# Seven-product merge and output projections in a one-core hybrid mixer layer

## The chip, the core and the metric

The kernel runs on one NeuronCore of a Trainium2 chip. The metric is device time in microseconds (us). Five engines matter here: TensorE multiplies matrices (PE in the profile; its weight loads are PEld), VectorE (DVE) and ScalarE (ACT) do elementwise work and read TensorE's results out of PSUM, GpSimd (POOL) takes some small work, and SyncE (SP) issues nearly all DMAs, in order.

## What is computed

One layer with width 1024 and sequence length 1024, all in float32, is computed transposed: channels lie on partitions, time on the free dimension.

```
h   = rms_norm(x, g) * (1 + scale(c)) + shift(c)        # scale, shift: rows of silu(c) @ ada_w
z   = h @ w_in                                          # q,k,v,z of three mixers + 3 x 1024 gate logits
y_b = mixer_b(z) * silu(z_b)                            # stick-breaking (sb), gated DeltaNet (gdn), GLA
m   = sum over b of sigmoid(gate_b) * (y_b @ proj_b)    # y_sb, y_gdn 512 wide, y_gla 1024 wide
out = x + gate(c) * (m @ w_out)
```

DeltaNet and GLA normalise their output per head with a learned scale (the "onorm" scale) ahead of the multiplication with silu(z_b).

## The kernel before, in words

**Exactness.** A float32 operand is cut into a high and a low part (`split`, L149: ScalarE rounds the high part at L151, VectorE subtracts at L152; with a column of scales L154 and L155 do it). A product is three matmuls: high·high, high·low, low·high. One matmul of the dense work takes a 128x128 stationary block and streams 128x512 through it. So a projection of 128 output channels with 1024 inputs over 1024 time steps costs 2 halves × 8 × 3 = 48 matmuls, one with 512 inputs 24 (`run_cm`, L187).

**Start.** The squares of x are summed over partitions by matmuls with ones (`add_up`, L316); VectorE adds some pairs first (L322, L329, L334). Two ScalarE steps (L336, L337) make the RMS factor `rstd`. The conditioning rows scale and shift of channel block k come for k = 0, 1 from 32 one-column matmuls on TensorE (`by_product`, L360, added up at L366), for k = 2 to 7 from VectorE reductions of an `ada_w` tile with silu(c) (`by_rows`, L369; L372, L374). Then for each k VectorE scales x (L404), ScalarE makes `h_hi` (L407) and VectorE `h_lo` (L409), and TensorE runs a block of 24 matmuls (eight accumulators in eight PSUM banks) on it while the next k is made.

**Middle.** `emit` (L247) weaves the three mixers, written as tasks with the names of what must be done before them, into a list of dense groups that fills TensorE's gaps. Of the 24 merge gates (3 branches × 8 blocks) 18 are computed early (`EARLY`, `FILL`, `early_gate`, L220) and stored in `g_dram`; they are fetched again later. The mixers store y in `y_dram`.

**Final stage** (`final_groups`, L1310). Eight GLA projections over the first 512 inputs are copied to `merged`. Then for GLA's second half, gdn and sb: eight projections each (`proj_group`, L1257), between them the gates, fetched or computed (six of them here). VectorE multiplies by the gate and adds into `merged` (L1267 to L1272). With the sb branch `merged` is split into `m_hi`, `m_lo`, and eight output projections follow (`out_group`, L1288): VectorE adds x (L1303), SyncE stores (L1306). The onorm scales are put into the projection weights: 96 pairs of L154/L155 on 128x128 pieces. `wp` holds three raw weight tiles and three split tiles.

## Time and profile before

| | us |
|---|---|
| Three runs | 1512.1, 1510.86, 1512.94; median 1512.1 |
| Profiled execution | 1507.79, of which the span is 1506.0 |
| TensorE busy | 1467.5 of 1506.0 |
| VectorE / ScalarE / GpSimd busy | 844.5 / 679.5 / 150.5 |
| Mean granted TensorE clock | 0.99 of full speed |

The span is the time between the first and the last instruction; 1.8 us of the execution lie around it. TensorE's busy time is from modelled ends, and consecutive matmuls overlap in the records, so the price of a matmul is read from the distance between starts, not from its length. In rows of the timeline the bracket gives the engine's idle time just before and what ended it.

### The profile page before, as it was taken

The page shows a single profiled execution, that of the slowest core. Times are in us where ns is not written, and L with a number is a line of the kernel's source. Part 1 is how long each engine was busy: PE and PEld are TensorE (multiplying, and loading weights), DVE is VectorE, ACT ScalarE, POOL GpSimd, SP SyncE. Part 2 cuts the span into 40 slices and gives each one's busy share as a digit, 9 for nine tenths or more (in the row PEclk, how much of TensorE's full clock was granted, in tenths as well). Part 3 has the DMA queues.
Part 4 walks back from the last instruction along what each step waited for, and adds up shares of the span by engine and source line. Part 5 has one row for each costly group of instructions (what it writes and reads, how often), then busy time and mean ns, then how long its engine had stood idle before and what let it go on. Part 6 is the DMA issues. An engine that isn't in the chain of part 4 may idle for free.

```text
span 1506.0 us, 26643 instructions
## 1 busy us (share of the span) xinstructions
PE 1467.5 (97%) x10628; PEld 1235.0 (82%) x10628; DVE 844.5 (56%) x1838; ACT 679.5 (45%) x1471; POOL 150.5 (10%) x295
## 2 busy tenths in 40 slices
PE   7998999989999999999999999999999999999998
PEld 4887777777778888879788999889988888888887
DVE  4978647476643756667576525563556226474621
ACT  5367645453743747465577423341433442322200
POOL 1021232133321000000000100000000000000000
PEclk8999999999999999999999999999999999999999
DMA  7634332131330212121122121111122234353442
GB/s 272 187 101 123 94 86 61 50 90 33 104 90 27 54 50 71 29 57 44 53 57 65 50 64 43 50 42 50 35 83 92 86 104 140 119 154 112 117 142 77
DMA packets 162470, 126.48 MB, mean 84 GB/s; under 512 B 23429, under 2 KB 139269, under 8 KB 162346
## 3 DMA queue, kind: packets, MB, share of 16 engines
q1 hardware_dynamic: 162202, 124.47, 28.6%
q8 instruction: 83, 1.36, 0.4%
q14 instruction: 41, 0.34, 0.1%
q10 hardware_dynamic: 144, 0.31, 0.1%
HBM read 99.80 MB, written 24.95 MB: 83 GB/s over the span
## 4 chain that ended last, share of the span: by engine, by line
PE 83%; DVE 8%; ACT 3%; DMA 3%; POOL 2%; issue 2%; SPq 0%; POOLq 0%; DVEq 0%; ACTq 0%
PE acc L95 66%; PE lv L95 7%; PE mx L95 6%; PE tr L122 2%; DVE u L436 1%; PE tr L95 1%; DVE w L621 1%; DVE w L623 1%; DVE w L152 1%; POOL w L647 1%; POOL c L284 1%; DMA w<-ad 1%; DMA w<-xd 1%; DVE u L1161 1%; DMA u<-in_xT 0%
## 5 line engine op out<-in xcount | busy, mean ns | idle before, releaser
L95 PE MATMUL acc<-h_hi,w 128*128 128x512 f32 x1856 | 656.4, 408 | 0.0
L95 PEld LDWEIGHTS acc<-h_hi,w 128*128 128x128 f32 x1856 | 352.0, 190 | 70.2 <-issue 0.2
L95 PE MATMUL acc<-h_lo,w 128*128 128x512 f32 x928 | 365.3, 394 | 1.8 <-DVE h_lo L409 1.8
L95 PEld LDWEIGHTS acc<-h_lo,w 128*128 128x128 f32 x928 | 176.8, 190 | 29.2 <-DVE h_lo L409 2.3
L95 PE MATMUL acc<-whi,h_hi 128*128 128x256 f32 x640 | 186.8, 292 | 0.0
L95 PE MATMUL acc<-wlo,h_hi 128*128 128x256 f32 x640 | 180.7, 282 | 0.0
L95 PE MATMUL acc<-whi,h_lo 128*128 128x256 f32 x640 | 180.7, 282 | 0.0
L95 PE MATMUL acc<-u,w 128*128 128x512 f32 x768 | 176.5, 391 | 0.0
L95 PEld LDWEIGHTS acc<-u,w 128*128 128x128 f32 x768 | 144.1, 188 | 31.7 <-ACT v L1226 0.2
L151 ACT CAST w<-raw 128x512 fp32r<-128x512 f32 x144 | 84.9, 619 | 131.8 <-PE acc L95 90.4
L152 DVE TENSOR_TENSOR w<-raw,w 128x512 fp32r<-128x512 f32 x144 | 97.5, 688 | 46.5 <-ACT w L151 46.0
L95 PEld LDWEIGHTS acc<-whi,h_hi 128*128 128x128 f32 x640 | 122.3, 191 | 1.4 <-issue 0.7
L95 PEld LDWEIGHTS acc<-wlo,h_hi 128*128 128x128 f32 x640 | 122.5, 191 | 0.1
L95 PEld LDWEIGHTS acc<-whi,h_lo 128*128 128x128 f32 x640 | 122.2, 191 | 0.0
L284 POOL TENSOR_TENSOR c<-c,mhalf 128x4 f32<-128x4 f32 (+1 forms) x56 | 55.0, 982 | 582.8 <-DVE c L282 581.4
L95 PE MATMUL acc<-m_hi,w 128*128 128x512 f32 x256 | 79.1, 389 | 0.0
L1161 DVE TENSOR_TENSOR_SCAN u<-u,zero_c 128x128 f32<-128x128 f32 (+7 forms) x32 | 43.4, 1356 | 35.5 <-ACT u L1159 35.5
L155 DVE SCALAR_TENSOR_TENSOR w<-raw,col,w 128x128 fp32r<-128x128 f32 x96 | 29.5, 349 | 55.7 <-ACT w L154 48.9
L95 PEld LDWEIGHTS mx<-r,u 128*128 128x128 f32 x288 | 44.1, 190 | 18.1 <-DVE r L802 5.2
L95 PEld LDWEIGHTS acc<-m_hi,w 128*128 128x128 f32 x256 | 48.1, 188 | 10.1
L95 PE MATMUL mx<-r,u 128*128 128x128 f32 x288 | 48.4, 280 | 6.3 <-POOL u L771 2.3
L95 PE MATMUL lv<-u,u 128*32 128x32 f32 (+5 forms) x528 | 48.9, 251 | 2.6 <-DVE u L704 2.6
(258 smaller groups left out, 2154.7 us busy)
## 6 DMA issues: line engine op xcount, KB each, us to landing
raw<-in_w_in SPq DMA_DIRECT2D x160, 256.0 KB, 3.0
g_dram<-v SPq DMA_DIRECT2D x36, 256.0 KB, 2.1
v<-g_dram SPq DMA_DIRECT2D x36, 256.0 KB, 2.7
u<-in_xT SPq DMA_DIRECT2D x16, 512.0 KB, 4.7
u<-y_dram SPq DMA_DIRECT2D x16, 512.0 KB, 3.7
ada<-in_adaT SPq DMA_DIRECT2D x12, 512.0 KB, 5.2
u<-in_adaT SPq DMA_DIRECT2D x8, 512.0 KB, 4.0
v<-gam_d SPq DMA_DIRECT2D x16, 256.0 KB, 3.6
```

The lines of the kernel that those rows point to most:

```text
L95: return nc.tensor.matmul(out, lhsT=lhsT, rhs=rhs, **kw)
L122: nc.tensor.transpose(out=out, in_=in_, identity=ident[:k, :k])
L151: nc.scalar.copy(out=hi, in_=raw)
L152: nc.vector.tensor_sub(out=lo, in0=raw, in1=hi.bitcast(F32))
L155: nc.vector.scalar_tensor_tensor(out=lo, in0=raw, scalar=scale, in1=hi.bitcast(F32), op0=ALU.mult, op1=ALU.subtract)
L284: nc.gpsimd.tensor_tensor(out=out, in0=out, in1=mhalf[:, 0:n], op=ALU.pow)
L436: nc.vector.scalar_tensor_tensor(out=t, in0=r[:, tap:tap + T], scalar=C("conv", j + tap), in1=t, op0=ALU.mult, op1=ALU.add)
L621: nc.vector.tensor_tensor(out=t3, in0=L3[:, w:16, j:w].broadcast_to([32, n, w]), in1=Xl3[:, j:w, 0:w].broadcast_to([32, n, w]), op=ALU.mult)
L623: nc.vector.tensor_sub(out=Xl3[:, w:16, 0:w], in0=Xl3[:, w:16, 0:w], in1=t3)
L647: nc.gpsimd.tensor_scalar(out=dst[:, :, 16 * e:16 * e + 16], in0=c3, scalar1=K("par")[:, e:e + 1], scalar2=None, op0=ALU.mult)
L1161: nc.vector.tensor_tensor_scan(om[:, 0:n][:, ::-1], om[:, 0:n][:, ::-1], zero_c.broadcast_to([P, n]), 1.0, ALU.mult, ALU.add)
```

## The change

Lines of the changed program are named with "new".

- **Seven products.** Output blocks p and p + 4 of the GLA projection, and of the output projection, are made together. With weights and inputs seen as 2x2 blocks (inputs 0 to 511 and 512 to 1023; time halves), seven block products in Winograd's form replace eight. VectorE forms s1 to s4 from the raw weights (`part`, new L1264 to L1272) and each is split; the input side has the units b11, t1, t2, b22, t3, b21, t4. A unit is 12 matmuls; two PSUM banks X and W take turns, and a bank is read in the middle of its accumulation (`read`) ahead of the unit after the next.
- **Input sums.** GLA's t1 to t4 are formed by four tasks `T.y` in the middle of the program: 16 loads of 128x512 from `y_dram`, 16 VectorE subtractions, 16 stores. Those of the output projection are formed from `merged` between the sb projections (`out_operands`, new L1449).
- **Final order.** All 24 gates go through `g_dram`. The six late ones come first in the final stage, then four GLA pairs, 16 gdn and sb projections in alternation, four output pairs. Operands are loaded into the low half's place and split there (`load_unit`, `load_y`).
- **Onorm scales** are multiplied in when y is made (40 instructions become scalar_tensor_tensor with a scalar column); the 96 pairs of L154/L155 on weights go.
- **Start.** All conditioning rows by VectorE, two more reductions for each of k = 0, 1; one more VectorE addition of squares (new L339, L340) and two ones-matmuls fewer; eight products of a constant with ones whose result nothing reads (`keep_busy`), three ahead of the squares and five behind them.
- Weight tiles: six of half the size, eight raw tiles instead of three.

```diff
-EARLY = [(g, d) for g in (1, 0, 2) for d in range(2, KT)]
+EARLY = [(g, d) for g in (1, 0, 2) for d in range(KT)]
...
-    wp = ctx.enter_context(tc.tile_pool(name="wp", bufs=3))
+    wp = ctx.enter_context(tc.tile_pool(name="wp", bufs=6))
...
+    idle = bank(pt, "tr", HALF)
+
+    def keep_busy(n):
+
+        for _ in range(n):
+            mm(idle, ones, cst[:, 0:HALF], 858, start=True, stop=True)
+
+    keep_busy(3)
...
-        return wp.tile([P, 4, P], F32, tag="raw", name="raw")
...
+        return wp.tile([P, 4, P], F32, tag="raw", name="raw", bufs=8)
+
+    def w_tile():
+        return wp.tile([P, 2, 4, P], F32R, tag="w", name="w")
...
+    def load_half(hi, lo, src, k0):
+        split(hi, lo, load_raw(src, k0))
+
+    def load_w(src, kt=KT):
+        ws = []
         for k0 in range(0, kt, 4):
-            load_half(w[:, 0, k0:k0 + 4, :], w[:, 1, k0:k0 + 4, :], src, k0, scales)
-        return w
+            w = w_tile()
+            load_half(w[:, 0], w[:, 1], src, k0)
+            ws.append(w)
+        return ws
...
-    nc.vector.tensor_add(out=low[1], in0=low[1], in1=low[2])
-    add_up(low[1], start=True)
-    add_up(low[0])
+    nc.vector.tensor_add(out=low[0], in0=low[0], in1=low[1])
+    nc.vector.tensor_add(out=low[0], in0=low[0], in1=low[2])
+    add_up(low[0], start=True)
...
-    PRE = 2
+    keep_busy(5)
...
-        if k < PRE:
-            for i, t in enumerate(tiles):
-                nc.sync.dma_start(out=t, in_=adaP[2 * k + i])
-            return lambda: by_product(k, tiles)
...
-    def by_product(k, tiles):
-        for i, t in enumerate(tiles):
-            at = 2 * k + i
-            for kk in range(KT):
-                mm(first_mod[:, at:at + 1], t[:, kk * P:(kk + 1) * P], c_col[:, kk:kk + 1], 120,
-                   start=(kk == 0), stop=(kk == KT - 1))
-        nc.vector.tensor_add(out=both(mod, k), in0=first_mod[:, 2 * k:2 * k + 2],
-                             in1=both(C("ada_b", 0, 24), k))
...
-    for k in range(PRE):
+    for k in range(KT):
         conds[k]()
-    for k in range(KT):
-        if k >= PRE:
-            conds[k]()
-        w = wp.tile([P, 2, 4, P], F32R, tag="w", name="w")
+        w = w_tile()
...
-        nc.vector.tensor_mul(out=y, in0=ps.rearrange("p c t -> p (c t)"), in1=st["z"][:, sl])
+        nc.vector.scalar_tensor_tensor(out=y, in0=ps.rearrange("p c t -> p (c t)"),
+                                       scalar=C("gdn_onorm"), in1=st["z"][:, sl],
+                                       op0=ALU.mult, op1=ALU.mult)
...
+        o = O_MG + gi * D + d * P
+        return (lambda: load_w(w_in[:, o:o + P])), (lambda w: run_cm(w, evac(), soon=early_part))
...
+    PRODUCTS = ("11", "s1", "s2", "s4", "s3", "12", "22")
+    UNITS = ("b11", "t1", "t2", "b22", "t3", "b21", "t4")
+
+    def strassen(src1, src2, rhs, prepare, read):
+
+
+        def load():
+            a = {}
+            for key, k0, src in (("11", 0, src1), ("21", 0, src2), ("22", 4, src2), ("12", 4, src1)):
+                a[key] = load_raw(src, k0)
+            ws = []
+            ahead.append(lambda: ws.append(part(a, len(ws))))
+            return a, ws, prepare()
+
+        def part(a, i):
+            key = PRODUCTS[i]
+            if key == "s1":
+                a["s1"] = raw_tile()
+                nc.vector.tensor_add(out=a["s1"], in0=a["21"], in1=a["22"])
+            elif key == "s2":
+                a["s2"] = raw_tile()
+                nc.vector.tensor_sub(out=a["s2"], in0=a["s1"], in1=a["11"])
+            elif key == "s4":
+                nc.vector.tensor_sub(out=a["s2"], in0=a["12"], in1=a["s2"])
+                a["s4"] = a["s2"]
+            elif key == "s3":
+                nc.vector.tensor_sub(out=a["21"], in0=a["11"], in1=a["21"])
+                a["s3"] = a["21"]
+            w = w_tile()
+            split(w[:, 0], w[:, 1], a[key])
+            return w
+
+        def run(loaded):
+            a, ws, context = loaded
+            ahead.pop(0)
+            while len(ws) < 3:
+                ws.append(part(a, len(ws)))
+            X, W = bank(pa, "acc", HALF), bank(pa, "acc", HALF)
+            for i, unit in enumerate(UNITS):
+                if i + 3 < 7:
+                    ws.append(part(a, i + 3))
+                else:
+                    early_part()
+                ps = X if i in (0, 2, 4, 6) else W
+                first, last = i in (0, 1, 5), i in (3, 5, 6)
+                n = 0
+                for p in range(4):
+                    for v, r in ((0, 0), (0, 1), (1, 0)):
+                        mm(ps, ws[i][:, v, p, :], rhs[p][unit][r], 216,
+                           start=(first and n == 0), stop=(last and n == 11),
+                           skip_group_check=True)
+                        n += 1
+                    if p == 1:
+                        yield
+                read(i, ps, context)
+                yield
+        return load, run
...
+    def differences(n, p, get):
+        def sub(out, a, b, t):
+            nc.vector.tensor_sub(out=out, in0=a, in1=b)
+            nc.sync.dma_start(out=t_dram[n, p][t], in_=out)
+
+        b12, b11 = get(flat(raw_tile()), 0, 1), get(flat(raw_tile()), 0, 0)
+        sub(b11, b12, b11, "t1")
+        b22 = get(flat(raw_tile()), 1, 1)
+        sub(b12, b22, b12, "t3")
+        sub(b22, b22, b11, "t2")
+        b21 = get(flat(raw_tile()), 1, 0)
+        sub(b21, b21, b22, "t4")
...
+            if i < 3:
+                r = c[i] = mid("v3" if i == 1 else "v2")
+                nc.scalar.copy(out=r, in_=ps)
+                return
+            b = {3: (0, 1), 4: (1, 1), 5: (0, 0), 6: (1, 0)}[i]
+            if i < 6:
+                r = c[{3: 2, 4: 1, 5: 0}[i]]
+                nc.vector.tensor_add(out=r, in0=r, in1=ps)
+            else:
+                r = ps
+            nc.vector.tensor_mul(out=block(p, *b), in0=c["g"][b[0]][b[1]], in1=r)
+        return strassen(*(proj_gla[:, d * P:(d + 1) * P] for d in (p, p + 4)), gla_c, dict, read)
...
+                t = mid("v4")
+                nc.vector.tensor_mul(out=t, in0=g[hf], in1=ps)
+                nc.vector.tensor_add(out=merged[d][:, sl], in0=merged[d][:, sl], in1=t)
+                for piece in pieces[:2]:
+                    piece()
+                del pieces[:2]
+            yield from run_cm(w, evac, ys[yi], 4, soon=early_part)
+            if gi == 0 and d >= 4:
+                out_operands(d - 4)
...
+        def put(name, src):
+            hi, lo = out_c[p][name] = new_unit(next(tags))
+            split(hi, lo, src)
+
+        def form(name, tag, a, b):
+            def piece():
+                src = t[name] = mid(tag)
+                nc.vector.tensor_sub(out=src, in0=a() if callable(a) else a,
+                                     in1=b() if callable(b) else b)
+                put(name, src)
+            return piece
+
+        pieces.extend([lambda: put("b11", b11), form("t1", "v2", b12, b11),
+                       form("t2", "v3", b22, lambda: t["t1"]), lambda: put("b22", b22),
+                       form("t3", "v2", b22, b12), lambda: put("b21", b21),
+                       form("t4", "v4", b21, lambda: t["t2"])])
...
+        def read(i, ps, xr):
+            b = {0: (0, 0), 1: (1, 1), 2: (0, 1), 3: (0, 1), 4: (1, 1), 5: (0, 0), 6: (1, 0)}[i]
+            x, d = xr[b[0]][b[1]], ds[b[0]]
+            w = HALF // 2 if p == 3 and i == 6 else HALF
+            for t0 in range(0, HALF, w):
+                ts = slice(t0, t0 + w)
+                nc.vector.scalar_tensor_tensor(out=x[:, ts], in0=ps[:, ts],
+                                               scalar=mod[:, 16 + d:17 + d], in1=x[:, ts],
+                                               op0=ALU.mult, op1=ALU.add)
+                if i >= 3:
+                    t1 = b[1] * HALF + t0
+                    nc.sync.dma_start(out=outT[d * P:(d + 1) * P, t1:t1 + w], in_=x[:, ts])
+        return strassen(*(w_out[:, d * P:(d + 1) * P] for d in ds), out_c, prepare, read)
...
+        gs = [gate(*e) for e in EARLY[sum(FILL):]]
+        gs[0] = after(lambda: gla_operands(FIRST_UNITS), gs[0])
+        gs += [after(lambda: gla_operands(("t3", "b21", "t4")), gla_pair(0))]
+        gs += [gla_pair(p) for p in range(1, 4)]
+        for branch, pairs in ((1, (0,)), (0, (0,)), (1, (1,)), (0, (1,)), (1, (2, 3)), (0, (2, 3))):
+            gs += [proj_group(branch, proj_gdn if branch else proj_sb, 4 * branch, d)
+                   for p in pairs for d in (p, p + 4)]
+        gs += [out_pair(p) for p in range(4)]
+        return [(g, ["S.m3"]) for g in gs]
...
+    for p in range(4):
+        tasks.append((f"T.y{p}", lambda p=p: y_differences(p), ["L.s3.1", f"D.S{min(p, 2)}"], 0))
```

By the program's order TensorE's matmuls of 128x512 in the GLA and output projections go from 768 to 672 (per pair 84 in place of 96), and between the first blocks and the last task of the mixers its order is the same as before. The following rows show three places.

**TensorE, end of the output projection** (m_hi, m_lo: the split of `merged`; w: weights; acc: a PSUM bank). First before, then with the change:

```order
L95 MATMUL acc_15138<-m_hi_14315,w_15043 128x512
L95 MATMUL acc_15138<-m_lo_14316,w_15043 128x512
L95 MATMUL acc_15138<-m_hi_14315,w_15043 128x512
L95 MATMUL acc_15138<-m_hi_14360,w_15043 128x512
L95 MATMUL acc_15138<-m_lo_14361,w_15043 128x512
L95 MATMUL acc_15138<-m_hi_14360,w_15043 128x512
```

```order
L95 MATMUL acc_15262<-unit_14294,w_15282 128x512 x3
L95 MATMUL acc_15262<-u5_14487,w_15282 128x512 x3
L95 MATMUL acc_15262<-u2_14773,w_15282 128x512 x3
L95 MATMUL acc_15262<-u3_14831,w_15282 128x512 x3
L95 MATMUL acc_15263<-unit_14297,w_15298 128x512 x3
L95 MATMUL acc_15263<-u7_14490,w_15298 128x512 x3
L95 MATMUL acc_15263<-u2_14776,w_15298 128x512 x3
L95 MATMUL acc_15263<-u3_14834,w_15298 128x512 x3
L95 MATMUL acc_15262<-unit_14318,w_15314 128x512 x3
L95 MATMUL acc_15262<-u8_14511,w_15314 128x512 x3
L95 MATMUL acc_15262<-u8_14810,w_15314 128x512 x3
L95 MATMUL acc_15262<-u4_14839,w_15314 128x512 x3
```

Before, one bank takes 24 such matmuls before it is read; now a bank is read after 12, the other bank's 12 lie between, and each three matmuls take one operand of a pair.

**VectorE, start** (tr: conditioning products of TensorE in PSUM; mod: conditioning rows; ada, u8: a tile of ada_w and silu(c); amp, u0: scale and x). First before, from the last addition of squares; then with the change, from the row of k = 0 (its two reductions stand just ahead):

```order
L334 TENSOR_TENSOR u3_156<-u3_156,u3_158 128x512 x2
L366 TENSOR_TENSOR mod_129<-tr_171,col_86 128x2
L399 SCALAR_TENSOR_TENSOR amp_170<-mod_129,col_86 128x1
L404 SCALAR_TENSOR_TENSOR u0_90<-u0_90,amp_170,u5_161 128x512
L152 TENSOR_TENSOR w_224<-raw_176,w_224 128x512
L404 SCALAR_TENSOR_TENSOR u0_90<-u0_90,amp_170,u5_161 128x512
L366 TENSOR_TENSOR mod_129<-tr_171,col_86 128x2
L399 SCALAR_TENSOR_TENSOR amp_170<-mod_129,col_86 128x1
L404 SCALAR_TENSOR_TENSOR u0_92<-u0_92,amp_170,u5_161 128x1024
L409 SCALAR_TENSOR_TENSOR h_lo_229<-u0_90,mod_129,h_hi_228 128x512 x2
```

```order
L376 TENSOR_TENSOR mod_131<-mod_131,col_86 128x2
L398 SCALAR_TENSOR_TENSOR amp_171<-mod_131,col_86 128x1
L403 SCALAR_TENSOR_TENSOR u0_90<-u0_90,amp_171,u5_162 128x512
L158 TENSOR_TENSOR w_198<-raw_181,w_198 128x512
L403 SCALAR_TENSOR_TENSOR u0_90<-u0_90,amp_171,u5_162 128x512
L374 ISA ada_183,mod_131<-ada_183,u8_120 128x1024
...
L374 ISA ada_184,mod_131<-ada_184,u8_120 128x1024
...
L408 SCALAR_TENSOR_TENSOR h_lo_203<-u0_90,mod_131,h_hi_202 128x512 x2
```

The additions that waited for TensorE are gone; the reductions of k = 1 now stand ahead of the first `h_lo`.

**VectorE, start of the output projection** (acc of L1475: an output bank being read; unit, u3, v: operands of the pair p = 3 being formed and split; w: weights). First before, then with the change:

```order
L1271 TENSOR_TENSOR v2_14634<-v1_14550,acc_14621 128x512
L152 TENSOR_TENSOR w_14708<-raw_14709,w_14708 128x512
L1272 TENSOR_TENSOR u8_13101<-u8_13101,v2_14634 128x512
L152 TENSOR_TENSOR w_14708<-raw_14713,w_14708 128x512
L152 TENSOR_TENSOR m_lo_14638<-u8_13101,m_hi_14637 128x1024
L1303 SCALAR_TENSOR_TENSOR v3_14677<-acc_14652,mod_129,u3_14603 128x512
L1303 SCALAR_TENSOR_TENSOR v3_14705<-acc_14680,mod_129,u3_14603 128x512
```

```order
L158 TENSOR_TENSOR unit_14818<-v2_14816,unit_14818 128x512
L158 TENSOR_TENSOR u8_14810<-v4_14808,u8_14810 128x512
L1449 TENSOR_TENSOR v3_14821<-u7_13910,v2_14816 128x512
L1475 SCALAR_TENSOR_TENSOR v0_14743<-acc_14858,mod_131,v0_14743 128x512
L1449 TENSOR_TENSOR v2_14829<-u7_13910,unit_13909 128x512
L158 TENSOR_TENSOR unit_14823<-v3_14821,unit_14823 128x512
L158 TENSOR_TENSOR unit_14826<-u7_13910,unit_14826 128x512
L158 TENSOR_TENSOR u3_14831<-v2_14829,u3_14831 128x512
L158 TENSOR_TENSOR u3_14834<-u7_13910,u3_14834 128x512
L1449 TENSOR_TENSOR v4_14837<-u7_13910,v3_14821 128x512
L158 TENSOR_TENSOR w_14878<-raw_14737,w_14878 128x512
L1475 SCALAR_TENSOR_TENSOR v3_14746<-acc_14859,mod_131,v3_14746 128x512
```

Before, an addition and three splits stood between the last gate multiplication (L1271) and the first read of an output bank, and the second read followed at once. Now seven instructions, operands and one weight split, stand between the reads of the first and the second unit; four more operand instructions and the last gate addition (new L1421) stand ahead of the first read, behind the last gate multiplication.

## Rows read from the trace of the kernel before

**Rows 1.** The page, parts 1 and 2: engines, and TensorE's clock by slice.

```profile
PE 1467.5 (97%) x10628; PEld 1235.0 (82%) x10628; DVE 844.5 (56%) x1838; ACT 679.5 (45%) x1471; POOL 150.5 (10%) x295
...
PEclk8999999999999999999999999999999999999999
```

**Rows 2.** The windows by stage; columns: stretch, then its length and each engine's busy us.

```profile
0.00:50.00 50.00, 39.64 (x152) 28.38 (x153) 29.54 (x50) 24.20 (x31) 4.63 (x19) 0.90 0.75 264
...
100.00:200.00 100.00, 92.64 (x562) 75.23 (x561) 68.33 (x204) 64.04 (x123) 17.50 (x41) 0.93 0.36 98
...
800.00:1110.00 310.00, 306.21 (x2327) 281.18 (x2326) 154.21 (x263) 124.03 (x350) 21.10 (x37) 1.00 0.19 54
...
1250.00:1300.00 50.00, 50.00 (x221) 41.11 (x220) 30.97 (x58) 15.38 (x35) 0.00 (x0) 1.00 0.49 143
...
1400.00:1450.00 50.00, 50.00 (x221) 41.28 (x220) 25.00 (x35) 11.06 (x16) 0.00 (x0) 1.00 0.43 126
...
1450.00:1506.00 56.00, 52.09 (x230) 42.81 (x228) 10.03 (x15) 2.29 (x4) 0.00 (x0) 0.98 0.31 99
```

**Rows 3.** The waits of TensorE: us in total, times, longest.

```profile
PE lv L95 <- DVE u L322: 4.4, 1, 4.4
...
PE acc L95 <- DVE h_lo L409: 1.8, 1, 1.8
```

**Rows 4.** The timeline of TensorE and VectorE, last 12 us: start, length.

```profile
1493.77 0.39 PE L95 MATMUL acc<-m_hi,w 128*128 128x512 f32 x1
...
1501.70 0.39 PE L95 MATMUL acc<-m_hi,w 128*128 128x512 f32 x1
...
1502.13 0.88 DVE L1303 SCALAR_TENSOR_TENSOR v<-acc,mod,u 128x256 f32<-128x256 f32 x2 [4.69 <-PE acc L95]
```

**Rows 5.** The timeline of VectorE in the output projection.

```profile
1459.28 1.28 DVE L152 TENSOR_TENSOR w<-raw,w 128x512 fp32r<-128x512 f32 x2
1464.05 0.75 DVE L1303 SCALAR_TENSOR_TENSOR v<-acc,mod,u 128x512 f32<-128x512 f32 x1 [3.49 <-PE acc L95]
```

**Rows 6.** The timeline of TensorE, 12 to 79 us.

```profile
12.05 9.11 PE L95 MATMUL lv<-u,ones 128*128 128x512 f32 x16 [4.36 <-DVE u L322]
...
30.46 0.77 PE L95 MATMUL acc<-h_hi,w 128*128 128x512 f32 x1
...
33.03 0.79 PE L95 MATMUL acc<-h_lo,w 128*128 128x512 f32 x1 [1.80 <-DVE h_lo L409]
...
35.33 0.63 PE L95 MATMUL mx<-h_hi,w 128*128 128x512 f32 x1
...
35.76 0.63 PE L95 MATMUL mx<-h_lo,w 128*128 128x512 f32 x1
...
72.67 0.39 PE L95 MATMUL acc<-h_hi,w 128*128 128x512 f32 x1
...
78.11 0.39 PE L95 MATMUL acc<-h_hi,w 128*128 128x512 f32 x1
```

**Rows 7.** The timeline of VectorE, 24 to 65 us.

```profile
24.66 0.16 DVE L366 TENSOR_TENSOR mod<-tr,col 128x2 f32<-128x2 f32 x1 [6.62 <-PE tr L95]
...
32.23 1.41 DVE L409 SCALAR_TENSOR_TENSOR h_lo<-u,mod,h_hi 128x512 fp32r<-128x512 f32 x2
...
34.16 1.22 DVE L372 CUSTOM_DVE_ANT_0 ada<-ada,u 128x1024 f32<-128x1024 f32 x1
...
43.77 1.28 DVE L409 SCALAR_TENSOR_TENSOR h_lo<-u,mod,h_hi 128x1024 fp32r<-128x1024 f32 x1
...
64.97 1.27 DVE L409 SCALAR_TENSOR_TENSOR h_lo<-u,mod,h_hi 128x1024 fp32r<-128x1024 f32 x1
```

**Rows 8.** The timeline of ScalarE: the last step of the RMS factor.

```profile
23.19 1.06 ACT L337 ACTIVATE u<-u 128x1024 f32<-128x1024 f32 x1
```

**Rows 9.** DMA issues: KB each, median us from issue to landing.

```profile
v<-g_dram SPq DMA_DIRECT2D x36, 256.0 KB, 2.7
...
u<-y_dram SPq DMA_DIRECT2D x16, 512.0 KB, 3.7
```

More of the change, by code (lines that the diff above doesn't have):

```diff
@@ L202, in run_cm @@
             evac(hf, sl, ps)
+            if hf == 0 and soon is not None:
+                for _ in range(3):
+                    soon()
             yield
@@ new lines, with fetch_gate @@
+    HS = [slice(hf * HALF, (hf + 1) * HALF) for hf in range(2)]
+    def fetch_gate(gi, d, tags):
+        gs = [mid(t) for t in tags]
+        for g, sl in zip(gs, HS):
+            nc.sync.dma_start(out=g, in_=g_dram[gi, d][:, sl])
+        return gs
+    PRODUCTS = ("11", "s1", "s2", "s4", "s3", "12", "22")
[50 more added lines that the diff above has]
+        return load, run
@@ new lines, in unit_tile, with new_unit, load_unit @@
+    def unit_tile(tag, dt=F32R):
+        if tag == "h":
+            return hp.tile([P, T], dt, tag="h", name="unit")
+        return mp.tile([P, 1032 if tag == "u0" else T], dt, tag=tag, name=tag,
+                       bufs=3 if tag == "u5" else 2)[:, 0:T]
+    def new_unit(tag):
+        u = unit_tile(tag)
+        return u[:, 0:HALF], u[:, HALF:]
+    def load_unit(tag, src):
+        hi, lo = new_unit(tag)
+        raw = lo.bitcast(F32)
+        nc.sync.dma_start(out=raw, in_=src)
+        nc.scalar.copy(out=hi, in_=raw)
+        nc.vector.tensor_sub(out=lo, in0=raw, in1=hi.bitcast(F32))
+        return hi, lo
```

218 lines of the change are left out of this document (106 added, 112 removed).

## The prediction

> **What bounds the kernel now.** I read the page first: TensorE is busy 97% of the span, VectorE 56%, ScalarE 45%, and TensorE's clock was granted in full in all but the first slice [rows 1]. A mean hides the stages, so the windows come next [rows 2]. There the reader should see three things. In the first 50 us TensorE idles 10.4 us at a mean clock of 0.90; from 100 to 200 us it idles 7.4 us at 0.93; in the last stage it is busy 50.00 of 50 us at 1.00, with VectorE at 25 to 31 us, until a tail of 3.9 us. So the last stage is bound by the number of matmuls and nothing else, and the start by what TensorE waits for. The waits name these for the start: squares added on VectorE (4.4 us) and the first `h_lo` (1.8 us) [rows 3]. Last, timelines give prices.
>
> The price of one 128x512 matmul is the distance of starts. From 1493.77 to 1501.70 us there are 35 distances: 7.93 / 35 = 0.2266 us [rows 4]. The windows agree: 50 / 220.5 = 0.2268 [rows 2]. I use 0.2267. At half clock it is 35.76 − 35.33 = 0.43 us [rows 6].
>
> **The change, part by part.**
>
> *Seven products.* Eight pairs lose 12 matmuls each: 96 × 0.2267 = 21.8 us. It all lies on TensorE's path, since TensorE never idles there [rows 2], and nothing takes its place on TensorE: sums, splits and reads are VectorE's and ScalarE's. The Trainium skill, "TensorE: Matmul & The Clock Gate", section "Back-to-back issue gap", gives about 131 ns per matmul of 512 columns in a sustained stream; by that figure the 96 would be worth an estimated 12.6 us. The trace does not agree: 0.2267 us, evenly. The sum goes by the trace.
>
> *Does VectorE keep up?* A unit lasts 12 × 0.2267 = 2.72 us, and its bank must be read before the unit after the next. Per pair of output blocks VectorE has 7 weight splits, 4 weight sums and 7 reads or gate steps, 18 instructions at 0.64 (half of 1.28) to 0.75 us [rows 5]: at most 13.5 us in 7 × 2.72 = 19.0. Each border costs nothing while less than 2.72 us of VectorE work stands between a unit's end and the read: read, split and sum are 0.75 + 0.64 + 0.64 = 2.0 us. The cover is thus 0.7 us per border. If it goes, a border costs what is over.
>
> *Start of the output projection.* Here it does go. After the last branch matmul (call its end E) VectorE does, in its order, the gate product (0.75), five instructions (5 × 0.64), the read of unit 1 (0.75), seven instructions (7 × 0.64) and the read of unit 2 (0.75): 9.9 us, and 0.2 us from TensorE's end to VectorE's start, as 1502.13 stands behind 1501.70 + 0.23 [rows 4]. Unit 2's bank is free at E + 10.1; unit 4 would start at E + 3 × 2.72 = E + 8.2. A stall of 2.0 us. At the ends: 0, if instructions overlap as chained ones do, to 3. I take 2.0, by the rows. At the other borders (GLA to branches, pair to pair) the same count leaves some 0.4 us, and I set them at 0.
>
> *Six gates ahead of the GLA pairs, 12 more gate stores and fetches, alternating branches.* The six gates are the same matmuls at another place: 0. They give 65 us of cover to the loads and splits of GLA's operands. A fetch of 256 KB lands in 2.7 us, one of 512 KB in 3.7 [rows 9]; gates have two buffers each, so a fetch is issued a whole projection (24 × 0.2267 = 5.44 us) ahead. DMA's share is below one half [rows 2]. Cost 0. Without that cover, 2.7 us for each late one.
>
> *Scales moved off the weights.* 96 pairs on ScalarE and VectorE go from the last stage, where both have slack: 0.
>
> *T.y in the middle.* 16 subtractions of about 0.64 us, 10 us in all, on a VectorE that is busy 154 of 310 us [rows 2]. But each waits for loads from `y_dram` (2.7 us for 256 KB [rows 9]), and behind it in VectorE's queue stand scans, splits and PSUM copies of the mixers, on which TensorE waits later. SyncE's queue also gets 32 transfers, a store behind each subtraction. Bounds: 0 below (nothing is removed there) and 4 tasks × 2.7 = 10.8 us. I take 1.5, near the lower end, because TensorE has dense work queued there and idles only 310 − 306.2 = 3.8 us [rows 2].
>
> *Start.* `rstd` is ready at 23.19 + 1.06 = 24.25, call it T0 [rows 8]. Before, VectorE then waited for TensorE's conditioning products (idle 6.62 us at 24.66) [rows 7], the first `h_lo` product started at 33.03 = T0 + 8.8, and the last first-stage block ended at 78.11 = T0 + 53.9 [rows 6]. After, VectorE has the row of k = 0 ready at T0. It scales two halves (0.71 each, half of 1.41) and splits a weight (0.64), does two reductions for k = 1 (2 × 1.22), then the first half of `h_lo` (0.71) [rows 5, 7]: T0 + 5.2, and T0 + 6.0 with the other half. For k = 1 to 7 follow seven times two passes of 1.28, a split of 0.64 and 0.3 of small ones, 3.5 us each, and 12 reductions of 1.22: 24.5 + 14.6. The last `h_lo` is there at T0 + 45.1, and 24 matmuls (78.11 − 72.67 = 5.44) [rows 6] end the stage at T0 + 50.5. So VectorE sets the pace throughout, and the gain is 53.9 − 50.5 = 3.4 us. T0 itself moves: two ones-matmuls fewer (9.11 / 8 = 1.14 us each [rows 6]) make it up to 2.3 us earlier, three filler products ahead and one more addition (at most 1.28) up to 4 us later. I leave it, and take 3.2 for the part; bounds −0.6 to 5.7.
>
> **Sum.** 21.8 + 3.2 − 2.0 − 1.5 = 21.5 us. The profiled execution took 1507.8 us, which would become 1486.3. It stands 4.3 us below the median of the three runs, 1512.1; against that median I predict 1512.1 − 21.5 = **1490.6 us**. What a measurement of this kernel can tell from no change is about 0.2%, 3.0 us.
>
> **The rivals.**
>
> *T.y holds up the mixers.* VectorE takes instructions in order, so four waits of a load each reach the chain of scans. For it: the subtractions stand between scans and copies. Against it: VectorE half idle, TensorE at 98.8% there [rows 2]. By the upper bound of 10.8 instead of 1.5: 1512.1 − (21.8 + 3.2 − 2.0 − 10.8) = 1499.9 us.
>
> *The 96 matmuls are worth only part of their price.* The 672 that are left could pass more slowly, because a bank changes hands after every 12 of them and not after 24. If each of the 56 units cost the 0.2 us of a hand-over between TensorE and VectorE [rows 4], 11.2 us come back: 1512.1 − (21.5 − 11.2) = 1501.8. Against it: banks change hands in the last stage now, and 220 to 221 matmuls pass in every 50 us all the same [rows 2]. The page's lower figure, named above, points the same way, and the trace speaks against it in the same row.
>
> *Slower: the borders of units bind.* There are 8 × 7 = 56 borders, each with a read on VectorE that may stand behind a split, which waits for ScalarE's cast, which waits for a raw weight. Saved are 21.8 + 3.2 − 1.5 = 23.5 us, so each border may cost 23.5 / 56 = 0.42 us before all is gone; that is, when VectorE has over 2.72 + 0.42 = 3.1 us between a unit's end and its read, against the 2.0 counted. With one more split and its wait (0.64 + 0.62 or so), 3.3 us stand there: 0.6 us of wait at each border, 33 us, and 1522 us. Waits also bear on the clock: the stretch from 100 to 200 us idles 7.4 us and was granted 0.93, the stretch from 800 to 1110 us idles 3.8 of 310 us and kept 1.00 [rows 2]; a unit wholly at half clock would take 12 × 0.2 = 2.4 us more. The Trainium skill, same page, section "HAM oscillation — how this bites in real kernels", says that gaps in TensorE's work put its clock back to half, time after time. By that rule this case would be dearer still; the trace shows it for the long idle stretch and not for the short waits.
>
> *More than forecast.* No stall at the output projection, T.y free, T0 earlier: 21.8 + 5.7 = 27.5 us, 1484.6.
>
> That the change does not take out the 96 matmuls is excluded: the order shows 672.
>
> **How the numbers follow.** Forecast 0.72 (its own range, from the bounds of the start, the stall and T.y's lower half, 1485 to 1498); T.y 0.12; products worth less 0.02; slower borders 0.07; borders in part, to no change, 0.04; more than forecast 0.03. The range reaches past the T.y case: **1485 to 1502**. Outside it lie the borders (0.11), the extra gain (0.03) and a little of T.y. Faster by more than 3.0 us: 0.72 + 0.12 + 0.02 + 0.03 = 0.89; same 0.04; slower 0.07.
>
> **What would show it.** Right: the windows of the last 300 us with TensorE at 50.0 of 50 but for one stretch near the output projection's start; 672 unit matmuls 0.227 us apart; first-stage blocks that each wait for `h_lo`, the stage's end near T0 + 50.5; TensorE's idle time in the mixers within 2 us of before. Wrong: a wait for a PSUM read at most unit borders, a granted clock under 1.00 in the last stage, or more waits of `mx` and `lv` products while T.y runs.

## The result and the profile after

The changed kernel takes 1486.2 us (median), the kernel before 1512.2, so 26.0 us less; the ratio is 0.9824 with a 95% interval of 0.9804 to 0.9843, 1.8% less. Forecast were 1490.6 us and 1485 to 1502. A second set of the same program gave 1485.0 us, 0.9839 (0.9820 to 0.9857). One of the four executions of the first set took 1750.4 us at a mean clock of 0.75; the median above counts it (without it, 1485.3 us), the ratio leaves it out. The profiled executions, whose parts are compared below, took 1507.8 and 1483.8 us: 24.0 us apart, as are their spans (1506.0 and 1482.0).

The page of the changed kernel, parts 1 and 2, as [rows 1]:

```profile
PE 1441.9 (97%) x10480; PEld 1206.6 (81%) x10480; DVE 918.8 (62%) x1914; ACT 697.9 (47%) x1470; POOL 151.5 (10%) x296
...
PEclk9999999999999999999999999999999999999999
```

TensorE is busy 25.6 us less, VectorE 74 us more, and TensorE's clock in the first slice reads 9 instead of 8. The windows, the stretches of [rows 2]:

```profile
0.00:50.00 50.00, 41.93 (x122) 25.98 (x123) 39.52 (x68) 25.50 (x33) 5.59 (x20) 0.93 0.88 304
...
100.00:200.00 100.00, 92.93 (x610) 75.40 (x608) 68.26 (x205) 62.43 (x130) 19.61 (x43) 0.98 0.35 95
...
800.00:1110.00 310.00, 306.17 (x2309) 281.18 (x2308) 168.13 (x283) 126.95 (x357) 21.09 (x37) 1.00 0.28 83
...
1250.00:1300.00 50.00, 50.00 (x220) 40.95 (x219) 27.33 (x42) 16.55 (x28) 0.00 (x0) 1.00 0.49 151
...
1400.00:1450.00 50.00, 48.95 (x212) 39.52 (x211) 37.92 (x58) 14.36 (x24) 0.00 (x0) 1.00 0.45 142
...
1450.00:1506.00 56.00, 28.23 (x123) 22.58 (x121) 12.28 (x18) 3.11 (x5) 0.00 (x0) 0.97 0.10 38
```

In the last stage TensorE no longer stands at 50.00 of 50: 1.05 us are idle from 1400 to 1450. In the 48.95 us that it is busy there, 212 matmuls pass; at 0.2267 us each 216 would. The tail after the last matmul is about as long as before (3.8 us against 3.9).

The whole is best cut at two marks which every run has: the end of the first stage (the start of the matmul after the last first-stage block: 78.11 in [rows 6], 73.33 below) and the first matmul of the last product of sb attention. The timeline of TensorE, first of the kernel before, then of the changed one:

```profile
1163.54 1.95 PE L95 MATMUL mx<-v,u 128*128 128x128 f32 x16
```

```profile
1156.88 1.95 PE L95 MATMUL mx<-v,u 128*128 128x128 f32 x16
```

| Profiled run | first stage ends | middle | final part, to the end of the span |
|---|---|---|---|
| before | 78.1 | 1085.4 | 1506.0 − 1163.5 = 342.5 |
| changed | 73.3 | 1083.6 | 1482.0 − 1156.9 = 325.1 |
| gain | 4.8 | 1.9 | 17.3 |

The 1.9 us of the middle are within what it scatters by (below).

### The profile page after: what moved, and what is told of

It is laid out like the page before. It is cut to its first block, busy times and chain, and to the rows that moved or that the text cites. A ratio compares the mean times of both kernels' runs of the same rounds, so it can differ in the third digit from the quotient of the medians.

```text
span 1482.0 us, 26690 instructions
## 1 busy us (share of the span) xinstructions
PE 1441.9 (97%) x10480; PEld 1206.6 (81%) x10480; DVE 918.8 (62%) x1914; ACT 697.9 (47%) x1470; POOL 151.5 (10%) x296
## 4 chain that ended last, share of the span: by engine, by line
PE 76%; DVE 12%; DMA 4%; ACT 3%; POOL 2%; issue 2%; SPq 0%; DVEq 0%; POOLq 0%; ACTq 0%
PE acc L95 62%; PE lv L95 5%; PE mx L95 5%; PE tr L122 2%; DVE w L158 2%; DVE w L625 1%; DVE ada L374 1%; DVE w L623 1%; DVE u L435 1%; DMA v<-gam_d 1%; POOL c L301 1%; POOL u L505 1%; DVE u L403 1%; DVE h_lo L408 0%; ACT w L157 0%
## 5 line engine op out<-in xcount | busy, mean ns | idle before, releaser
L157 ACT CAST w<-raw 128x512 fp32r<-128x512 f32 x232 | 141.8, 620 | 220.3 <-PE acc L95 192.0
L158 DVE TENSOR_TENSOR w<-raw,w 128x512 fp32r<-128x512 f32 x232 | 158.6, 691 | 129.4 <-ACT w L157 126.8
L95 PE MATMUL acc<-w,h_hi 128*128 128x256 f32 x1280 | 238.8, 287 | 0.0
L95 PEld LDWEIGHTS acc<-w,h_hi 128*128 128x128 f32 x1280 | 198.8, 191 | 1.5 <-issue 0.7
L95 PE MATMUL acc<-w,h_lo 128*128 128x256 f32 x640 | 180.8, 282 | 0.0
L95 PEld LDWEIGHTS acc<-w,h_lo 128*128 128x128 f32 x640 | 122.2, 191 | 0.0
L95 PE MATMUL acc<-unit,w 128*128 128x512 f32 x312 | 79.8, 393 | 1.1 <-DVE v L1475 1.1
L1224 ACT ACTIVATE v<-acc,col 128x512 f32<-128x512 f32 x48 | 33.0, 687 | 83.9 <-PE acc L95 83.4
L95 PEld LDWEIGHTS acc<-unit,w 128*128 128x128 f32 x312 | 58.4, 188 | 14.8 <-DVE v L1475 1.5
L95 PEld LDWEIGHTS lv<-u,u 128*32 128x32 f32 (+2 forms) x528 | 40.1, 145 | 11.2 <-issue 6.7
```

The source lines that it names most:

```text
L95: return nc.tensor.matmul(out, lhsT=lhsT, rhs=rhs, **kw)
L157: nc.scalar.copy(out=hi, in_=raw)
L158: nc.vector.tensor_sub(out=lo, in0=raw, in1=hi.bitcast(F32))
L1224: nc.scalar.activation(out=g, in_=ps, func=AF.Identity, bias=C("merge_b", gi * 8 + d))
```

## The experiments

Each is an edit of one of the two kernels, with times of its own comparison, in which the kernel before had medians of 1508.5 to 1510.9 us; so ratios are compared, and the parts of the table above. The parts of all profiled runs:

| Run | median us | ratio (95%) | first stage ends | middle | final part |
|---|---|---|---|---|---|
| e1_start_alone | 1504.8 | 0.9957 (0.9939 to 0.9974) | 74.1 | 1088.0 | 342.4 |
| e3_old_start | 1490.0 | 0.9859 (0.9838 to 0.9880) | 81.6 | 1084.9 | 324.3 |
| e4_eight_out | 1494.6 | 0.9889 (0.9870 to 0.9908) | 74.2 | 1082.7 | 334.9 |
| e5_reads_and_gates_first | 1482.6 | 0.9813 (0.9793 to 0.9833) | 74.3 | 1085.9 | 323.6 |
| e2_no_fillers | 1487.7 | 0.9860 (0.9841 to 0.9880) | 75.2 | 1083.2 | 324.7 |
| e6_1_more_per_unit | 1487.7 | 0.9860 (0.9844 to 0.9877) | 74.3 | 1086.5 | 325.2 |
| e6_2_more_per_unit | 1491.9 | 0.9890 (0.9875 to 0.9904) | 74.0 | 1085.0 | 331.5 |
| e7_no_input_sums | 1484.6 | 0.9838 (0.9823 to 0.9853) | 74.3 | 1084.1 | 325.0 |
| c1_changed_again | 1485.0 | 0.9839 (0.9820 to 0.9857) | 74.2 | 1083.4 | 324.8 |
| e9_shifted | 1483.1 | 0.9822 (0.9803 to 0.9841) | 74.2 | 1082.5 | 325.0 |

**The start alone** (on the kernel before):

```diff
-    PRE = 2
-    first_mod = bank(pt, "tr", HALF)
+    keep_busy(5)
...
-    for k in range(PRE):
-        conds[k]()
     for k in range(KT):
-        if k >= PRE:
-            conds[k]()
+        conds[k]()
```

> The kernel before with the new start alone: all conditioning rows by VectorE reductions, eight filler products, one more VectorE addition of squares, two ones-matmuls fewer. Theory (the start gives 4.8 us at the end of the first stage, 78.1 to 73.3 us, and all of it and no less is passed on to the end): 1512.2 - 4.8 to 6.7 = 1505.5 to 1507.4 us, with the first stage ending near 73.3 us in the trace. Rival A (the forecast's size, 3.2 us): 1509. Rival B (what the start gives is lost again in the stretch from 78 to 340 us, and the lead there comes from the larger raw and weight buffers): first stage ends near 73.3, but the time is over 1510.

Measured: 6.0 us less, 0.9957. The first stage ends at 74.1 and the final part is that of before to 0.1 us. The middle of this profile is 2.6 us longer, so part of the start's gain is not seen in that one execution; in the median it is. The size is above the forecast's 3.2 us and within the theory's range; the interval (3.9 to 9.2 us) leaves out rival A, and rival B falls.

**The old start in the changed kernel** (the reverse edit; `by_product` as in the kernel before):

```diff
-    keep_busy(3)
...
-    keep_busy(5)
+    PRE = 2
+    first_mod = bank(pt, "tr", HALF)
...
+        if k < PRE:
+            for i, t in enumerate(tiles):
+                nc.sync.dma_start(out=t, in_=adaP[2 * k + i])
+            return lambda: by_product(k, tiles)
```

> The changed kernel with the start of the kernel before (32 one-column conditioning products on TensorE, no fillers); the seven products and all else stay. Theory: the final stage's 17.3 us stay and the start's 4.8 to 6.7 us go: 1486.2 + 4.8 to 6.7 = 1491 to 1493 us. Rival (start and products are worth what the forecast said, 3.2 and 18.3): 1489.4. If it stays under 1488, the start is worth nothing and the lead in the middle comes from the buffers.

Measured: 0.9859, final part 324.3. By ratio the rest of the change is worth 1.41% and the start what is missing to 0.9824 or 0.9839, 3 to 5 us with some 3 us of uncertainty. The median of 1490.0 lies between the theory's 1491 and the rival's 1489.4 and does not tell them apart. The old start itself varies: its first stage ended at 78.1 in one profile and at 81.6 in the other. The clock differs with it: TensorE was granted 0.50, the level of 1.2 GHz, from 26.3 to 36.5 us in the first and from 24.0 to 41.1 in the second.

**No fillers:**

```diff
-    keep_busy(3)
...
-    keep_busy(5)
```

> The changed kernel without the eight filler products (their result is read by nothing). Theory (VectorE paces the first stage, the fillers only raise TensorE's clock ahead of it): the RMS factor comes 1 to 2 us later, since six ones-matmuls run at half clock, and the first stage ends 1 to 2 us later: 1487.2 to 1488.2 us. Rival A (the fillers do nothing): 1486.2, the first stage ends at 73.3 as now. Rival B (without them the whole first stage falls to half clock): over 1490.

The first stage ends at 75.2 in the one profile without fillers, against 73.3 to 74.3 in nine profiles with them: about 1 us. The time alone (1487.7) could not tell it. TensorE's timeline without fillers, then that of the changed kernel:

```profile
12.41 8.62 PE L95 MATMUL lv<-u,ones 128*128 128x512 f32 x12 [4.95 <-DVE u L339]
...
25.71 0.79 PE L95 MATMUL acc<-h_hi,w 128*128 128x512 f32 x1 [4.69 <-ACT h_hi L404]
...
29.18 0.79 PE L95 MATMUL acc<-h_lo,w 128*128 128x512 f32 x1 [2.67 <-DVE h_lo L406]
```

```profile
7.51 5.28 PE L95 MATMUL tr<-cst,ones 128*128 128x512 f32 x6
...
15.38 3.70 PE L95 MATMUL lv<-u,ones 128*128 128x512 f32 x8 [0.87 <-DVE u L346]
...
18.92 4.45 PE L95 MATMUL tr<-cst,ones 128*128 128x512 f32 x10
...
27.24 0.79 PE L95 MATMUL acc<-h_lo,w 128*128 128x512 f32 x1 [2.97 <-DVE h_lo L408]
...
73.33 0.39 PE L95 MATMUL acc<-h_hi,w 128*128 128x512 f32 x1
```

With fillers four sums of squares (x8 records) take 3.70 us, 0.93 each; without them six (x12) take 8.62, 1.44 each. The engine had waited 4.95 us ahead of them in the one and multiplied constants in the other. The constants themselves pass at 5.28 / 6 = 0.88 us a record at first and at 4.45 / 10 = 0.445 later, about twice as fast. One microsecond of the windows, without fillers and then with them:

```profile
16.00:17.00 1.00, 0.99 (x2) 1.00 0.99 365
```

```profile
16.00:17.00 1.00, 1.00 (x4) 1.00 1.01 371
```

Two records against four, and the view gives a clock of 1.00 for both. That figure is no measurement here: the first record of the granted clock in the trace begins at 18.5 us without fillers and at 12.5 us with them (at 16.1 us in the kernel before), and the view reads 1.00 where there is no record. At just these times, within one record, the distance of starts falls from 0.85 to 0.43 us in each of the three. So the products ahead of the first record passed at the half rate, and with fillers the full rate, 2.4 GHz, came 6 us earlier. For the same reason the 0.90 and 0.93 of the first 50 us in the windows are too high.

The five fillers behind the squares did not hold it. TensorE waits 2.97 us for the first `h_lo` (27.24 above) and is then granted 0.50, the level of 1.2 GHz, here in the changed kernel:

```profile
27.00:32.90 5.90, 5.66 (x13) 4.45 (x14) 5.90 (x12) 2.20 (x4) 0.10 (x1) 0.50 1.07 363
```

The Trainium skill, "TensorE: Matmul & The Clock Gate", section "HAM oscillation — how this bites in real kernels", says that idle gaps put the clock back to half; this row agrees, with 0.50 behind a wait of 2.97 us.

**Eight products in the output projection:**

```diff
-        return strassen(*(w_out[:, d * P:(d + 1) * P] for d in ds), out_c, prepare, read)
+        return eight(*(w_out[:, d * P:(d + 1) * P] for d in ds), out_c, prepare, read)
...
+            for i, (r_, j) in enumerate(((0, 0), (0, 1), (1, 1), (1, 0))):
...
+                for q in range(2):
+                    for p in range(4):
+                        for v, r in ((0, 0), (0, 1), (1, 0)):
+                            mm(ps, ws[2 * r_ + q][:, v, p, :], rhs[p][f"b{q + 1}{j + 1}"][r], 216,
+                               start=(n == 0), stop=(n == 23))
```

> The changed kernel with eight block products in place of seven in the output projection alone (96 matmuls for each pair of output blocks, a bank read once after 24; four splits of merged and of weights in place of seven, no sums). 48 matmuls come back: 48 x 0.2267 = 10.9 us. Theory (the seven-product output projection loses about 1.2 us in a stall at its start and 0.004 us on each of 336 matmuls, 1.3 us): the eight-product form gives these back, 1486.2 + 10.9 - 2.5 = 1494.6 us. Rival A (borders cost nothing): 1497.1. Rival B (borders of units bind, most of the gain of the products is lost there): under 1491.

The final part grows by 9.8 us (334.9 against 325.1). So in the output projection 48 matmuls less are worth 9.8 of 10.9 us. The median, 1494.6, is just the theory's figure, but that is partly luck: the theory's own difference is 10.9 − 2.5 = 8.4 us, and one of its two reasons does not hold. With eight products the matmuls of the output projection start as far apart as with seven (48 of them take 1433.86 − 1422.78 = 11.08 us, 0.231 each), so the stall at its start is given back and the distances are not.

```profile
1422.78 0.85 PE L95 MATMUL acc<-u,w 128*128 128x512 f32 x3
...
1433.86 0.86 PE L95 MATMUL acc<-u,w 128*128 128x512 f32 x3
```

GLA and the branches have the rest of 17.3, by subtraction: 342.5 − 334.9 = 7.6 of 10.9.

**Reads and gates first:**

```diff
+            g = fetch_gate(gi, d, ("v0", "v1"))
             if yi not in ys:
                 ys[yi] = load_y(yi)
-            g = fetch_gate(gi, d, ("v0", "v1"))
...
-                for piece in pieces:
+                for piece in pieces[:-4]:
                     piece()
+                del pieces[:-4]
...
-                       form("t3", "v2", b22, b12), lambda: put("b21", b21),
+                       form("t3", "v4", b22, b12), lambda: put("b21", b21),
...
         def read(i, ps, xr):
...
+            if pieces:
+                pieces.pop(0)()
```

> The changed kernel with two things put in another order: the last four operand pieces of pair p = 3 (b22, t3, b21, t4) are formed between the bank reads of the first output pair instead of ahead of them, and a projection's gate is fetched ahead of the y tiles in SyncE's queue. Theory: the two stalls of TensorE in the final stage (1.23 us at 1407, 0.79 us at 1309 us) go: 1486.2 - 2.0 = 1484.2 us, and no wait over 0.3 us stands in the trace of the final stage. Rival (the next instruction is late in their place: a weight split or a y split): 1485.5 to 1486.5, with a new wait of 1 us or more at either place.

TensorE's waits in the final part, first of the changed kernel, then of this one, then of the same with all tiles shifted (e9_shifted, below):

```profile
PE acc L95 <- DVE v L1475: 1.1, 1, 1.1
...
PE acc L95 <- DVE v L1420: 0.5, 1, 0.5
```

```profile
PE acc L95 <- DVE v L1420: 0.4, 1, 0.4
```

```profile
PE acc L95 <- DVE v L1420: 1.3, 1, 1.3
```

The wait for the bank read (L1475) is gone in both; the wait for the gated product (L1420) is not: 0.5 becomes 0.4 in one and 1.3 us in the other. So the first edit does what was expected and the second does not. The second moved nothing: through the first branch projections SyncE issues its transfers in the same order, by their tiles, in the traces of the changed kernel and of this one: seven of the eight y tiles ahead of the first gate fetch for the branches in both. What holds the gate up is its buffer. SyncE's timeline and waits (1300 to 1316 us) and VectorE's timeline, in the changed kernel:

```profile
1310.31 0.34 SPq L1240 DMA_DIRECT2D v<-g_dram  x1
```

```profile
SPq L1240 <- DVE unit L1391: 5.6, 2, 4.1
```

```profile
1309.60 0.68 DVE L1391 TENSOR_TENSOR unit<-v,v 128x512 f32<-128x512 f32 x1
```

The fetch that VectorE waits for at L1420 is issued at 1310.31, 0.03 us after the last GLA pair's gate product (L1391) has let go of the buffer, and lands 4.5 us later, where such a fetch has a median of 2.9 in this kernel. In the two reordered runs it is issued just as closely behind L1391 and takes 4.4 and 5.2 us. What lengthens it from 2.9 us is not shown. Both versions with this order have medians of 1482.6 and 1483.1 us, some 2 us under the changed kernel; the intervals overlap, the final part of one (323.6) is 1.5 us shorter.

**One and two VectorE instructions more per unit** (`range(1)`, then `range(2)`; the residual is written again):

```diff
             split(w[:, 0], w[:, 1], a[key])
+            for _ in range(1):
+                nc.vector.tensor_sub(out=w[:, 1], in0=a[key], in1=w[:, 0].bitcast(F32))
```

> The changed kernel with one more VectorE instruction of 128x512 (0.6 us) at each of the 56 weight splits of the seven-product units; it writes the same low half again. Theory (a border between units has about 0.7 us of cover): almost all of it is hidden, 1 to 2 us more at the two places where TensorE already waits: 1487 to 1488.5 us. Rival (borders of units bind already): 56 x 0.6 = 34 us more at most, and over 1500 us.

> The same with two more instructions, 1.25 us per unit. Theory (0.7 us of cover): now the borders bind. VectorE's 18 instructions per pair become 32, about 20.2 us against 19.04 us of matmuls, and each border is over its cover by up to 0.55 us: 8 x 1.2 = 9 us to 56 x 0.55 = 31 us more, 1495 to 1517 us, with TensorE waiting for bank reads at many borders. Rival (the cover is larger, VectorE is not near): under 1490 us.

One more costs nothing: final part 325.2, and the same two waits. Two more cost 6.4 us (331.5), less than the 9 of the lower bound. The waits of the final part with one, then with two:

```profile
PE acc L95 <- DVE v L1477: 1.1, 1, 1.1
...
PE acc L95 <- DVE v L1422: 0.6, 1, 0.6
```

```profile
PE acc L95 <- DVE v L1477: 3.8, 1, 3.8
...
PE acc L95 <- DVE w L1277: 1.2, 2, 0.6
```

Of the 6.4 us, 2.7 are the longer wait at the output projection's start (3.8 us against 1.1). Some 2.8 more are the clock: behind the wait of 3.8 us TensorE is granted 0.50, the level of 1.2 GHz, and 12 matmuls start 0.43 us apart, where behind the wait of 1.1 us it kept 1.00 (1400 to 1450 us in the windows above). The last 1 us are two waits for a weight split (L1277), less the gate wait, which is not among the waits here. The windows with two instructions more:

```profile
1409.00:1415.60 6.60, 5.74 (x14) 4.54 (x15) 5.89 (x11) 0.19 (x1) 0.00 (x0) 0.50 0.17 54
```

So the borders have cover for one instruction more (0.6 us), and the rival by which borders bind already is out. With two (1.25 us) nearly all borders are still covered, so the theory's 0.7 us is too small for most of them; it said waits at many borders, and the view lists three.

**No input sums:**

```diff
-                    src = t_dram["y", p][name]
+                    alt = {"t1": "b12", "t2": "b22", "t3": "b22", "t4": "b21"}[name]
+                    src = y_dram[8 + p + 4 * (alt[1] == "2")][:, HS[alt[2] == "2"]]
...
-    for p in range(4):
-        tasks.append((f"T.y{p}", lambda p=p: y_differences(p), ["L.s3.1", f"D.S{min(p, 2)}"], 0))
```

> The changed kernel without the four T.y tasks: the input sums t1 to t4 of the GLA projection are left out (16 loads, 16 subtractions, 16 stores less), and the seven-product units read plain blocks of y in their place. Theory (the sums cost the mixers 0.7 us, the fall of the lead over the kernel before from 7.4 to 6.7 us at the end of the middle): 1485.4 us, with the lead staying at 7.4. Rival A (the forecast's 1.5 us or more): 1484.7 or less. Rival B (its upper bound): 1475. Under 0.5 us of difference: the sums cost nothing.

The middle takes 1084.1 us without the sums. With them it takes 1082.5 to 1086.5 in nine profiles of kernels whose middle is the same program. The sums cost nothing that can be seen against this; the theory's 0.7 us and the forecast's 1.5 are neither shown nor excluded, and rival B's 10.8 is out.

**The changed kernel again, and all tiles shifted** (the second is "reads and gates first" with this edit on top):

```diff
-                   dynamic_dma_scratch_size=1024)
+                   dynamic_dma_scratch_size=4096)
```

> The changed kernel once more, nothing edited, as a second profile. Theory (from the start of S.m3's last products to the end the time is fixed by the program, and the middle scatters by some 2 us between executions of the same instructions): final part 325.1 us within 0.4 us, first stage ending at 73.3 to 74.3 us, the middle anywhere from 1082.5 to 1087 us. Rival (the middle's differences come from the edits of the runs): a middle of 1083.5 us again, within 0.3 us.

> The reordered kernel (reads and gates first) with all tiles moved by 3072 bytes in each partition of SBUF, by a larger scratch area at its start; nothing else. In the output projection a unit of 12 matmuls takes 2.77 us where 12 x 0.2267 = 2.72, evenly over the 12, and a branch projection 5.56 where 5.44. Theory A (the tiles' places in SBUF set this): the spacing changes, and the final part with it, by 1 to 4 us from 323.6. Theory B (it is not the place): the final part stays at 323.6 us within 0.4, and the time at the changed kernel's less 1.2 to 2 us.

The repeat's final part agrees to 0.3 us. Its middle, 1083.4, agrees with the first one's as well, so by itself it does not show scatter; the nine profiles with this middle do, 1082.5 to 1086.5 us, and so does e1's against that of before (1088.0 and 1085.4, the same program). Part of the scatter goes with the granted clock: it is at 0.50 for 20 us of e1's middle and 14 of the longest of the nine (e6_1), for 3 to 7 us of the three shortest; what else moves it is open.

In the shifted kernel the spacing in the branches is unchanged: 24 matmuls take 1352.18 − 1346.61 = 5.57 us, in the unshifted one 5.56 (1345.54 to 1351.10, below). TensorE's timeline of the shifted kernel:

```profile
1346.61 0.86 PE L95 MATMUL acc<-unit,w 128*128 128x512 f32 x3
...
1352.18 0.86 PE L95 MATMUL acc<-unit,w 128*128 128x512 f32 x3
```

So theory A, that the place in SBUF sets the spacing, fails for a common shift. Its final part of 325.0 is not the expected 323.6: 0.9 us of the difference are the longer gate wait above (1.3 us against 0.4), the rest short waits in GLA.

## Why the prediction was right, and where its terms were off

The time lies in the range, and the main mechanism was the one forecast: fewer matmuls in a stage that TensorE bounds. The start became shorter as forecast, but VectorE does not pace it, so the forecast of its end came close partly by luck. The gain was 26.0 us against 21.5: the products gave less than forecast (17.3 against 19.8), the start more, and T.y's cost was not seen.

- **Seven products, 21.8 − 2.0 forecast, 17.3 measured.** TensorE gave back more than the one stall: 4.4 us of the 21.8, added up under the price of a matmul below. The stall at the output projection came where it was placed, 1.1 us and not 2.0. VectorE's and TensorE's timeline there:

```profile
1402.89 0.75 DVE L1475 SCALAR_TENSOR_TENSOR v<-acc,mod,v 128x512 f32<-128x512 f32 x1
...
1407.77 0.75 DVE L1475 SCALAR_TENSOR_TENSOR v<-acc,mod,v 128x512 f32<-128x512 f32 x1
...
1408.57 0.97 PE L95 MATMUL acc<-unit,w 128*128 128x512 f32 x3 [1.05 <-DVE v L1475]
```

With the first matmul behind it, which is slower, the stall costs 1.3 us. The reads of unit 1 and unit 2 are 4.88 us apart, with the seven instructions of the forecast between them, and TensorE starts unit 4 after 1.05 us of idling. The chain is shorter than counted since chained instructions follow each other by 0.60, not 0.64.
- **The borders set at 0.** Of GLA's end this was wrong. The step "a fetch is issued a whole projection ahead" failed for the first projection: the gate buffers are held by the last GLA pair, so the fetch goes out at 1310.31, when the projection has already begun (1309.43). VectorE waits for the gate, and TensorE then stands idle for the 0.5 us of the wait on L1420 above (0.8 us with the slower starts beside it). The forecast had the buffers and did not ask who holds them.

```profile
1314.92 0.69 DVE L1420 TENSOR_TENSOR v<-v,acc 128x512 f32<-128x512 f32 x1 [0.63 <-DMA v<-g_dram]
```

- **The price of a matmul.** The step took 0.2267 us for the matmuls that are left. That is the distance in the gates and in the output projection before; in the GLA and branch projections of the kernel before it is already (32.66 − 0.39) / 141 = 0.229 us, with 0.39 the length of one:

```profile
1315.65 32.66 PE L95 MATMUL acc<-u,w 128*128 128x512 f32 x142
```

With the change it is 0.229 in the GLA pairs and 0.231 from the branches on. The period of a unit in the output projection is (1456.07 − 1439.43) / 6 = 2.77 us, not 2.72; two halves of a branch projection take 1351.10 − 1345.54 = 5.56, not 5.44; a GLA pair takes 1270.79 − 1251.55 = 19.24, not 19.04. VectorE's reads, then TensorE's starts, then GLA's:

```profile
1439.43 0.75 DVE L1475 SCALAR_TENSOR_TENSOR v<-acc,mod,v 128x512 f32<-128x512 f32 x1 [0.65 <-PE acc L95]
...
1456.07 0.75 DVE L1475 SCALAR_TENSOR_TENSOR v<-acc,mod,v 128x512 f32<-128x512 f32 x1 [1.41 <-PE acc L95]
```

```profile
1345.54 0.86 PE L95 MATMUL acc<-unit,w 128*128 128x512 f32 x3
...
1351.10 0.86 PE L95 MATMUL acc<-unit,w 128*128 128x512 f32 x3
```

```profile
1251.55 13.26 PE L95 MATMUL acc<-u,w 128*128 128x512 f32 x57
...
1270.79 13.26 PE L95 MATMUL acc<-u,w 128*128 128x512 f32 x57
```

Summed over all starts of 128x512 matmuls in the final part, 1476 before and 1380 with the change, the 4.4 us are 2.4 us at waits (1.3 and 0.8 at the two places above, 0.3 at shorter ones) and 2.1 us of wider distances; the shorter tail gives 0.1 back. It is the rival of products worth less, in a small size and by another way: starts lie further apart evenly, not at the borders. The lower figure of the Trainium skill, which the prediction names, is not borne out by any of it.
- **Start, 3.2 forecast, 4.8 in the profile and 6.0 in the median of the start alone.** The first stage ends at 73.3 in this profile, at 74.0 to 74.3 in the eight others with the new start, so 4.8 is its largest gain (others 3.8 to 4.2). The factor is ready 2.1 us earlier than the 24.25 of [rows 8] (T0 = 22.18):

```profile
21.12 1.06 ACT L354 ACTIVATE u<-u 128x1024 f32<-128x1024 f32 x1
```

The first `h_lo` product starts at 27.24 = T0 + 5.1 (5.2 forecast, T0 + 8.8 before), so this part of the chain was right. The step "VectorE sets the pace throughout" was not. TensorE's waits in the first 82 us, its timeline, then VectorE's:

```profile
PE acc L95 <- DVE h_lo L408: 3.0, 1, 3.0
```

```profile
35.25 0.39 PE L95 MATMUL acc<-h_hi,w 128*128 128x512 f32 x1
...
67.89 0.39 PE L95 MATMUL acc<-h_hi,w 128*128 128x512 f32 x1
```

```profile
65.22 1.27 DVE L408 SCALAR_TENSOR_TENSOR h_lo<-u,mod,h_hi 128x1024 fp32r<-128x1024 f32 x1
```

TensorE waits for `h_lo` once and not at each block. From 35.25 on seven blocks follow each other at 5.44 us, 24 × 0.2267, and VectorE has the last `h_lo` ready at 66.49 = T0 + 44.3, 1.4 us before TensorE takes up the last block. So TensorE sets the pace, with VectorE close behind (the repeat shows one more wait, of 0.6 us), and T0 + 51.2 against the forecast's T0 + 50.5 is a near miss of two counts that happen to be close. The 4.8 us are 2.1 of T0's move and 3.7 of the chain to the first `h_lo`, less 1.0: the first block takes 35.25 − 27.24 = 8.0 us against 7.0 before, with 12 distances of 0.43 us, the half rate, where there were 6. T0's move, left at zero, goes with the fillers: 22.2 to 23.3 in the nine profiles with them, 24.12 without.
- **T.y, 1.5 forecast, nothing seen.** 1.5 us lie within the middle's scatter; TensorE is as busy from 800 to 1110 us as before (306.17 and 306.21).
- **The slower rival** needed over 0.42 us at each border. It is not near: with two instructions more at each of the 56 splits only three waits stand in the trace. Its remark on the clock is borne out at the longest of them (3.8 us, then 0.50).

## What to carry to other kernels

In a stage that TensorE fills, a matmul taken out is worth the distance of starts, so a seven-product form pays if the other engines have cover at each bank read: count the VectorE work between a unit's end and its read against one unit's matmuls (here 2.0 of 2.7 us; one instruction more was free, two cost 6.4 us, nearly all at one seam and in the half clock behind it). Look for the losses at the seams, where operands for the next phase are formed in a row ahead of the first reads, or where a buffer that the next phase needs first is held until the last read of the phase before. Ask of a figure that reads full whether the trace has a record there at all. Cut profiled runs at common marks before reading small differences: here the final part repeats within 0.8 us (324.3 to 325.1 in five profiles of the same instructions) and the middle scatters by 4.
